# Issuing the later modulation loads of a decoder layer from GpSimd's queue instead of SyncE's

## The chip, the cores and the metric

The kernel runs on one core of one Trainium2 chip. The metric is the device time of one execution in microseconds (us). The engines are TensorE (PE), VectorE (DVE), ScalarE (ACT), GpSimd (POOL) and SyncE (SP). Loads from memory are issued by an instruction on an engine's queue and carried by the core's 16 DMA engines.

## The reference

One decoder layer (DEPTH = 1) on x of 256 tokens by D_MODEL = 2048, in fp32: a modulation from the conditioning vector c, a gated DeltaNet mixer with 16 key heads and 32 value heads of 128, a layer norm, a SwiGLU of width 5632 and a second layer norm. What matters here:

```
cond = silu(c)
mod = cond @ mod_w + mod_b                 # 2048 -> 6 * 2048
sh1, sc1, ga1, sh2, sc2, ga2 = split(mod, 6)
h = x * (1 + sc1) + sh1
y = gated_deltanet(h, w_in, ...)           # starts with h @ w_in, 2048 -> 12352
x = layer_norm(ALPHA_DN * x + (1 + ga1) * y, ...)
h = x * (1 + sc2) + sh2
y = (silu(h @ w_gate) * (h @ w_up)) @ w_down
x = layer_norm(ALPHA_DN * x + (1 + ga2) * y, ...)
```

sc1 and sh1 are needed before anything can be multiplied with w_in. Each is a product of a vector with a 2048 x 2048 matrix.

## The kernel before, in words

Every large product is made of three fp32r passes. A weight tile of 128 x 1024 (two rows of 128 inputs by 512 outputs, 512 KB) is loaded into `raw` by SP (line 187), ACT copies it to the hi half `wh` (line 190), DVE subtracts to get the lo half `wl` (line 191), and PE multiplies (lines 223 to 225). There are four buffers each of raw, wh and wl. The activations h are split in the same way into `hT` (`affine_split`, lines 375 to 391): PE transposes x (line 380), ACT makes hi (387), DVE makes the value and the lo half (390, 391).

The first part of the kernel goes in four quarters over the 2048 inputs, 512 inputs in each, so that w_in can be started before the whole of sc1 and sh1 is known. For each quarter the loop at line 884 does this, in program order:

- `mods_first(k0, ...)` computes sc1 and sh1 for the quarter's 512 columns. It has eight units u of two loads each (line 297), a load being 128 inputs by 2 x 512 columns of mod_w (128 partitions with two rows of 2 KB, 512 KB). Its products are eight small matmuls for each load (line 311); in the quarters behind the first, units 1, 3 and 5 are accumulated by DVE instead (lines 305, 307) and folded in at line 315. `to_columns` (lines 277, 280) and lines 323 and 324 then write sc1 and sh1.
- two loads of x for the quarter, 256 KB each, on SP (line 888), and `affine_split` for its four tiles of inputs;
- six chunks of w_in, one of each group in `first`: two weight loads and 24 products of 512 columns each.

The buffers of the modulation loads are borrowed from tiles that are used later: unit u takes entry u mod 5 of `early` (o2, o3, kq, kq, LA; 1 MB each, two buffers in kq). So unit 5 reuses the buffer of unit 0, and unit 0 of the next quarter that of unit 5; a load waits until PE or DVE has consumed what was in its buffer.

What is issued in which order on each queue is fixed when the program is built. A planner takes the instructions that are ready by its own estimate of durations, the one with the lowest due time first. Due times are set by hand with `at(...)`: unit u of a quarter at t0 + 1.5 u, its products at t0 + 1.5 (u + 0.5), chunk i of the same quarter's loads at t0 + 12.75 + 1 + 2 i, products of the weights from 0 on, t0 beginning at -100 and growing by 12.75 for each quarter. Due times of a quarter's chunks and of the next quarter's modulation units so overlap, and SP's queue carries them interleaved. A queue is served in order: an instruction that waits holds up all behind it.

POOL issues the loads of the small parameters (`columns`, line 143, and lines 166 and 167), and later a few loads and stores and small arithmetic. After the quarters, `mods_late` loads the other modulation weights on SP (line 332).

Of the kernel before, what the change touches and what calls it, by code (L numbers as in the profile page):

```python
# [29 lines left out]
def gdn_layer_kernel(ctx: ExitStack, tc: tile.TileContext, x, c, mod_w, mod_b, ln_g, ln_b,  # L30
                     w_gu, w_down, w_in, conv_w, a_log, dt_bias, norm_w, w_out, out):
    nc = tc.nc
# [23 lines left out]
    @contextmanager  # L56
    def at(p):

        old = tc.cur_priority
        tc.cur_priority = int((p + 200) * 1000)  # L60
        yield
        tc.cur_priority = old
# [27 lines left out]
    def tp():  # L90
        return psum.tile([128, 512], F32, name="tp", tag="tp", bufs=2)
# [41 lines left out]
    p = tp()  # L133
# [16 lines left out]
    p = tp()  # L150
# [123 lines left out]
    def to_columns(p, hw, nb):  # L274

        acc = work.tile([128, 256], F32, name="sums", tag="hf", bufs=2)
        act(acc[:, 0:hw], p[:, 0:hw], AF.Copy)
        q = tp()
        for i in range(nb):
            mm(q[:, 4 * i:4 * i + 4], acc[:, i * 128:(i + 1) * 128], ident[:, 0:128:32], start=True, stop=True)  # L280
        return q[:, 0:4 * nb].rearrange("p (i j) -> p j i", j=4)

    mod_pairs = mod_w2.rearrange("(k p) (s c) -> p k s c", p=128, c=D)

    def mods_first(k0, nk, tags, t0, gap, by_dve):


        cols, hw = nk * 128, nk * 64
        per = 1024 // cols
        p = tp()  # L290
        rest = None
        for u in range(KT // per):
            pool, tag, n = tags[u % len(tags)]
            raw = pool.tile([128, per, 2 * cols], F32, name="mraw0", tag=tag, bufs=n)
            with at(t0 + gap * u):
                for kl in range(per):
                    nc.sync.dma_start(raw[:, kl].rearrange("p (s c) -> p s c", s=2),
                                      mod_pairs[:, per * u + kl, 0:2, k0 * 128:(k0 + nk) * 128])
            with at(t0 + gap * (u + 0.5)):
                for kl in range(per):  # L300
                    k = per * u + kl
                    if u in by_dve:
                        if rest is None:
                            rest = work.tile([128, 1024], F32, name="macc", tag="macc", bufs=1)
                            ts(rest[:, 0:2 * cols], raw[:, kl], cond[:, k:k + 1], None, op0=OP.mult)
                        else:
                            stt(rest[:, 0:2 * cols], raw[:, kl], cond[:, k:k + 1], rest[:, 0:2 * cols],
                                op0=OP.mult, op1=OP.add)
                        continue
                    for j in range(4):  # L310
                        mm(p[32 * j:32 * j + 32, 0:hw], cond[:, k:k + 1].to_broadcast([128, 32]),  # L311
                           raw[:, kl, j * hw:(j + 1) * hw], start=(k == 0), stop=(k == KT - 1))
                if rest is not None and u == max(by_dve) + 1:
                    for j in range(4):
                        mm(p[32 * j:32 * j + 32, 0:hw], ones.to_broadcast([128, 32]),
                           rest[:, j * hw:(j + 1) * hw], start=False, stop=False)
        with at(t0 + gap * (KT // per)):
            qv = to_columns(p, hw, nk // 2)

            def halves(a):  # L320
                return a[:, k0:k0 + nk].rearrange("p (h i) -> p h i", h=2)

            stt(halves(sc1), qv[:, 2:4], 1.0, halves(modb[:, 16:32]), op0=OP.add, op1=OP.add)
            tt(halves(sh1), qv[:, 0:2], halves(modb[:, 0:16]), op=OP.add)
# [559 lines left out]
    for k0 in range(0, KT, 4):  # L884
        mods_first(k0, 4, early, t0, MGAP, (1, 3, 5) if k0 else ())
        with at(t0 + 8.2 * MGAP):
            for t in range(2):
                nc.sync.dma_start(xt[t][:, k0 * 128:(k0 + 4) * 128],
                                  x2[t * 128:(t + 1) * 128, k0 * 128:(k0 + 4) * 128])
        with at(t0 + 8.2 * MGAP + 0.5):  # L890
            for k in range(k0, k0 + 4, 2):
                affine_split(xt, hT, k, sc1, sh1)
        t0 += 8.5 * MGAP
        for i, group in enumerate(first):
            group.chunk(k0, t0 + CGAP0 + CGAP * i)
# [228 lines left out]
```

## Time and profile before

| | |
|---|---|
| median of 3 runs | 1728.11 us (1725.67 to 1729.37) |
| the profiled execution | 1724.8 us, span 1723.0 us |
| PE busy in the span | 1668.4 us (97%) |
| DVE, ACT, POOL busy | 1140.0, 879.3, 49.0 us |
| DMA | 390.82 MB, 227 GB/s over the span |

A view by windows gives, for each stretch, the time for which each engine was busy, the granted TensorE clock as a share of full speed, the share of time for which the DMA engines were busy (it can pass 1), and what they moved. The timeline lists instructions in order of start, with equal neighbours merged. An entry in square brackets tells how long the engine was idle before and what ended that. PEld is PE's loading of weights.

### The profile page before, as it was taken

Reading aid. Unit: us, or ns where it says so; the run is one execution under the profiler, and the core shown is the slowest. Engines: PE = TensorE matmul, PEld = TensorE weight load, DVE = VectorE, ACT = ScalarE, POOL = GpSimd, SP = SyncE. Lnnn points to the kernel's source line nnn. Section 1 sums busy time; section 2 is a strip of 40 time slices with the busy share of each in tenths; the row PEclk is TensorE's granted clock in tenths of the full one; section 3 lists DMA queues with packets and bytes.
Section 4 is the critical chain, followed back from the end, with each engine's and each line's share of the span. In section 5 each row is a group of like instructions: output and inputs, shape, how many; then the busy total and the mean of one; then the engine's idle time right before and its main releaser. Section 6 shows DMA issues by size and latency. Waiting matters only on the chain.

```text
span 1723.0 us, 23257 instructions
## 1 busy us (share of the span) xinstructions
PE 1668.4 (97%) x8685; PEld 1325.3 (77%) x8685; DVE 1140.0 (66%) x1641; ACT 879.3 (51%) x1426; POOL 49.0 (3%) x58
## 2 busy tenths in 40 slices
PE   5999999999999999999999999999999999999996
PEld 2666777787887878787788778888878887888885
DVE  2466988958966988847776865764567444455455
ACT  2433669769568667564333734444444443433331
POOL 0000000001001000000000000000000000000000
PEclk8999999999999999999999999999999999999998
DMA  9998785535863777747888576886678666765653
GB/s 351 364 337 282 225 290 186 171 111 160 257 205 112 245 247 240 247 147 237 300 285 278 159 259 193 298 271 188 187 243 290 186 190 204 249 195 190 196 193 107
DMA packets 183938, 390.82 MB, mean 227 GB/s; under 512 B 12096, under 2 KB 14320, under 8 KB 182800
## 3 DMA queue, kind: packets, MB, share of 16 engines
q1 hardware_dynamic: 181808, 378.64, 67.5%
q0 software_dynamic: 2016, 10.68, 1.8%
q8 instruction: 68, 1.11, 0.3%
q14 instruction: 46, 0.38, 0.1%
HBM read 385.08 MB, written 4.19 MB: 226 GB/s over the span
## 4 chain that ended last, share of the span: by engine, by line
PE 71%; DVE 11%; DMA 8%; issue 5%; ACT 3%; POOL 1%; SPq 1%; DVEq 0%; POOLq 0%; ACTq 0%
PE pj L224 19%; PE pj L223 19%; PE pj L225 19%; DMA mraw<-in_mod_w_dram 6%; DVE wl L191 5%; DVE macc L272 1%; PE gd L225 1%; PE gd L224 1%; ACT wh L190 1%; PE gd L223 1%; PE tp L311 1%; DVE X L586 1%; DVE cy L470 1%; DVE tmp L584 1%; PE tp L1039 1%
## 5 line engine op out<-in xcount | busy, mean ns | idle before, releaser
L191 DVE TENSOR_TENSOR wl<-raw,wh 128x1024 fp32r<-128x1024 f32 x522 | 634.9, 1222 | 375.5 <-ACT wh L190 372.4
L190 ACT ACTIVATE wh<-raw 128x1024 fp32r<-128x1024 f32 x522 | 552.3, 1061 | 603.2 <-PE pj L225 480.9
L223 PE MATMUL pj<-wh,h2T 128*128 128x512 f32 x704 | 278.2, 395 | 0.0
L225 PE MATMUL pj<-wh,h2T 128*128 128x512 f32 x704 | 276.7, 393 | 0.0
L224 PE MATMUL pj<-wl,h2T 128*128 128x512 f32 x704 | 276.6, 393 | 0.0
L223 PE MATMUL pj<-wh,hT 128*128 128x512 f32 x640 | 256.9, 403 | 0.0
L224 PE MATMUL pj<-wl,hT 128*128 128x512 f32 x640 | 256.4, 401 | 0.1
L225 PE MATMUL pj<-wh,hT 128*128 128x512 f32 x640 | 256.2, 401 | 0.0
L272 DVE SCALAR_TENSOR_TENSOR macc<-mraw,cond,macc 128x1024 f32<-128x1024 f32 x120 | 153.4, 1278 | 55.8 <-DMA mraw<-in_mod_w_dram 55.4
L223 PEld LDWEIGHTS pj<-wh,h2T 128*128 128x128 f32 x704 | 132.8, 189 | 30.7 <-issue 1.6
L225 PEld LDWEIGHTS pj<-wh,h2T 128*128 128x128 f32 x704 | 132.7, 189 | 28.6 <-issue 0.8
L224 PEld LDWEIGHTS pj<-wl,h2T 128*128 128x128 f32 x704 | 132.7, 188 | 27.5 <-issue 0.8
L223 PEld LDWEIGHTS pj<-wh,hT 128*128 128x128 f32 x640 | 120.8, 189 | 26.6 <-issue 3.3
L225 PEld LDWEIGHTS pj<-wh,hT 128*128 128x128 f32 x640 | 120.9, 189 | 24.6 <-issue 1.2
L224 PEld LDWEIGHTS pj<-wl,hT 128*128 128x128 f32 x640 | 120.8, 189 | 24.4 <-DVE wl L191 0.9
L470 DVE SCALAR_TENSOR_TENSOR cy<-tp,cw,cy 128x255 f32<-128x255 f32 (+2 forms) x192 | 86.2, 476 | 1.3 <-ACT cy L466 1.2
L224 PE MATMUL gd<-wl,hT 128*128 128x512 f32 x128 | 51.5, 404 | 1.4 <-DVE wl L191 1.4
L223 PE MATMUL gd<-wh,hT 128*128 128x512 f32 x128 | 49.9, 398 | 2.0 <-DVE part L256 1.1
L225 PE MATMUL gd<-wh,hT 128*128 128x512 f32 x128 | 51.8, 408 | 0.0
L311 PE MATMUL tp<-mraw,cond 128*32 128x256 f32 x368 | 34.9, 464 | 11.1 <-DMA mraw<-in_mod_w_dram 11.1
L223 PE MATMUL pj<-wh,oTc 128*128 128x512 f32 x112 | 43.9, 392 | 0.0
L225 PE MATMUL pj<-wh,oTc 128*128 128x512 f32 x112 | 43.8, 391 | 0.0
(385 smaller groups left out, 2252.0 us busy)
## 6 DMA issues: line engine op xcount, KB each, us to landing
raw<-in_gdn_w_in_dram SPq DMA_DIRECT2D x194, 512.0 KB, 4.7
mraw<-in_mod_w_dram SPq DMA_DIRECT2D x192, 512.0 KB, 5.4
raw<-in_ffn_w_gu_dram SPq DMA_DIRECT2D x176, 512.0 KB, 4.4
raw<-in_ffn_w_down_dram SPq DMA_DIRECT2D x88, 512.0 KB, 4.7
raw<-in_gdn_w_out_dram SPq DMA_DIRECT2D x64, 512.0 KB, 5.0
x<-in_x_dram SPq DMA_DIRECT2D x8, 256.0 KB, 6.0
r<-in_x_dram POOLq DMA_DIRECT2D x2, 1024.0 KB, 5.1
x1s<-r POOLq DMA_DIRECT2D x2, 1024.0 KB, 6.7
```

The costliest lines, as they stand in the source:

```text
L190: act(hi, raw, AF.Copy)
L191: tt(lo, raw, f32(hi), op=OP.subtract)
L223: mm(ps, sh, wh, start=start, stop=False)
L224: mm(ps, sh, wl, start=False, stop=False)
L225: mm(ps, sl, wh, start=False, stop=stop)
L272: return stt(acc, w, cond[:, k:k + 1], acc, op0=OP.mult, op1=OP.add)
L311: mm(p[32 * j:32 * j + 32, 0:hw], cond[:, k:k + 1].to_broadcast([128, 32]), raw[:, kl, j * hw:(j + 1) * hw], start=(k == 0), stop=(k == KT ...
L470: stt(y[:, o + s:o + 256], p[:, o:o + 256 - s], tap(3 - s, ct + i), y[:, o + s:o + 256], op0=OP.mult, op1=OP.add)
L584: tt(tv, LD[:, j + 1:32, j:j + 1].to_broadcast([128, n, m]), X[:, j, None, 0:m].to_broadcast([128, n, m]), op=OP.mult)
L586: tt(X[:, j + 1:32, 0:m], X[:, j + 1:32, 0:m], tv, op=OP.subtract)
L1039: tr(p[:, i * 256 + t * 128:i * 256 + (t + 1) * 128], nats[j, t][:, (2 * i2 + i) * 128:(2 * i2 + i + 1) * 128], ident)
```

## The change

The queue of the modulation loads in `mods_first` is chosen by quarter: SP for the first (k0 = 0), POOL for the three others. Sizes, buffers and due times stay, and so do all other loads.

```
+        queue = nc.gpsimd if k0 else nc.sync
         for u in range(KT // per):
             pool, tag, n = tags[u % len(tags)]
             raw = pool.tile([128, per, 2 * cols], F32, name="mraw0", tag=tag, bufs=n)
             with at(t0 + gap * u):
                 for kl in range(per):
-                    nc.sync.dma_start(raw[:, kl].rearrange("p (s c) -> p s c", s=2),
-                                      mod_pairs[:, per * u + kl, 0:2, k0 * 128:(k0 + nk) * 128])
+                    queue.dma_start(raw[:, kl].rearrange("p (s c) -> p s c", s=2),
+                                    mod_pairs[:, per * u + kl, 0:2, k0 * 128:(k0 + nk) * 128])
```

## Rows read from the trace of the kernel before

**Rows 1.** Busy time by windows: head, quarters, the rest, the span.

```profile
0.00:40.00 40.00, 22.65 (x164) 7.32 (x165) 8.15 (x22) 7.53 (x11) 4.25 (x13) 0.90 0.96 346
40.00:170.00 130.00, 126.49 (x707) 86.15 (x706) 77.86 (x88) 46.74 (x59) 0.49 (x1) 0.99 0.93 330
170.00:1723.00 1553.00, 1519.26 (x7818) 1231.78 (x7816) 1053.97 (x1532) 825.01 (x1358) 44.26 (x44) 0.99 0.67 215
sum 1723.00, PE 1668.40 PEld 1325.25 DVE 1139.98 ACT 879.29 POOL 49.01; mean PE 556.13 PEld 441.75 DVE 379.99 ACT 293.10 POOL 16.34
```

**Rows 2.** The page's chain that ended last, by engine.

```profile
PE 71%; DVE 11%; DMA 8%; issue 5%; ACT 3%; POOL 1%; SPq 1%; DVEq 0%; POOLq 0%; ACTq 0%
```

**Rows 3.** Timeline of SP's queue, head: start us, us, line, what is issued.

```profile
1.65 17.95 SPq L297 DMA_DIRECT2D mraw<-in_mod_w_dram  x16
20.50 1.62 SPq L888 DMA_DIRECT2D x<-in_x_dram  x2
25.50 0.89 SPq L297 DMA_DIRECT2D mraw<-in_mod_w_dram  x2
26.43 1.40 SPq L187 DMA_DIRECT2D raw<-in_gdn_w_in_dram  x2
```

**Rows 4.** Timeline of PE, head.

```profile
24.39 1.04 PE L311 MATMUL tp<-mraw,cond 128*32 128x256 f32 x8 [0.21 <-DMA mraw<-in_mod_w_dram]
25.67 0.64 PE L311 MATMUL tp<-mraw,cond 128*32 128x256 f32 x8 [0.25 <-DMA mraw<-in_mod_w_dram]
...
29.54 0.64 PE L311 MATMUL tp<-mraw,cond 128*32 128x256 f32 x8 [0.65 <-DMA mraw<-in_mod_w_dram]
...
31.70 1.39 PE L380 MATMUL tp<-ident,x 128*128 128x128 f32 x7 [0.25 <-DVE sh L324]
...
36.53 1.94 PE L311 MATMUL tp<-mraw,cond 128*32 128x256 f32 x16
...
38.39 1.22 PE L223 MATMUL pj<-wh,hT 128*128 128x512 f32 x2
```

**Rows 5.** Timeline of ACT and DVE, head.

```profile
34.66 1.06 ACT L190 ACTIVATE wh<-raw 128x1024 fp32r<-128x1024 f32 x1 [0.24 <-DMA raw<-in_gdn_w_in_dram]
...
35.93 1.06 ACT L190 ACTIVATE wh<-raw 128x1024 fp32r<-128x1024 f32 x1 [0.21 <-DMA raw<-in_gdn_w_in_dram]
...
36.16 0.68 DVE L391 TENSOR_TENSOR hT<-hf,hT 128x512 fp32r<-128x512 f32 x1
...
36.96 2.35 DVE L191 TENSOR_TENSOR wl<-raw,wh 128x1024 fp32r<-128x1024 f32 x2
```

**Rows 6.** DMA issues from 31 to 40 us: KB each, median us to landing.

```profile
raw<-in_gdn_w_in_dram SPq DMA_DIRECT2D x4, 512.0 KB, 10.0
mraw<-in_mod_w_dram SPq DMA_DIRECT2D x4, 512.0 KB, 10.3
prow<-in_ln_g_dram POOLq DMA_DIRECT2D x1, 16.0 KB, 4.5
prow<-in_ln_b_dram POOLq DMA_DIRECT2D x1, 16.0 KB, 4.6
```

**Rows 7.** Timeline of POOL: two places where it issues loads.

```profile
36.89 0.50 POOL L143 DMA_DIRECT2D prow<-in_ln_b_dram  x1 [0.99 <-PE tp L146]
...
1466.26 2.13 POOL L1093 DMA_DIRECT2D l<-in_ln_g_dram  x4
```

**Rows 8.** What PE waited for, 36 to 170 us: total, times, longest.

```profile
PE gd L224 <- DVE wl L191: 1.4, 3, 0.6
PE gd L223 <- DVE part L256: 1.1, 2, 0.5
...
PE gd L223 <- DMA mraw<-in_mod_w_dram: 0.5, 1, 0.5
```

**Rows 9.** Two windows of 2 us, read for granted clock and DMA share.

```profile
38.00:40.00 2.00, 2.00 (x12) 1.32 (x5) 1.98 (x3) 0.00 (x0) 0.00 (x0) 0.50 1.05 404
...
42.00:44.00 2.00, 2.00 (x10) 1.64 (x9) 1.62 (x2) 1.41 (x2) 0.00 (x0) 0.92 1.05 407
```

**Rows 10.** The chain, 60 to 170 us: first product of the second quarter.

```profile
84.46 0.45 PE pj L223 x2
```

## The prediction

> **What bounds the kernel now.** I read the busy time by stage first [rows 1]. PE is busy 1668.4 of 1723.0 us. Before 40 us it is busy 22.65 of 40, so 17.4 us are idle there; from 40 to 170 us, where all four quarters of the first projections run, 126.49 of 130, so 3.5 us are idle; and 33.7 us are idle in the 1553 us behind that, which the change does not touch. The chain that ended last is PE for 71% of the span and DMA for 8% [rows 2]. So the change can win at most the 3.5 us of the quarters and what it moves in the head, and it can lose whatever it holds PE up for.
>
> The head is bound by transfers. SP issues the 16 loads of the first quarter by 19.6 us [rows 3]; PE's products with them follow one another at the pace of landing: load 11 (counted from 0) starts at 24.39, load 12 at 25.67, load 15 at 29.54 us [rows 4]. So one load of 512 KB takes (29.54 - 24.39) / 4 = 1.29 us when all DMA engines are busy (share 1.05 at 38 to 40 us [rows 9]). Behind load 15 come the sums, the transposes of x (31.70) and, on DVE, the split of h, which ends at 36.84 [rows 4, 5]. The first weights land at 34.66 and 35.93 (ACT starts on each then), DVE has the first lo half at about 38.13, and the first product starts at 38.39 [rows 4, 5]. From there PE hardly stops: its named waits from 36 to 170 us are 1.4 us for lo halves, 1.1 us for partial sums, 0.5 us for a modulation load [rows 8], and small ones.
>
> A quarter of transfers is 16 modulation loads, 12 weight loads and 1 load's worth of x: 29 x 1.29 = 37.4 us. A quarter of PE's work runs from 38.39 [rows 4] to 84.46 us [rows 10], 46 us. Once the quarters run, PE is the slower one, and transfers have 8 us to spare in each.
>
> **The change part by part.** Nothing is added or left out: 48 of the 64 loads go to POOL's queue, their sizes and buffers stay. POOL spends 0.50 us on an issue (2.13 us for four) [rows 7]; a load here has 256 rows of 2 KB where those have 128 rows, so 0.5 to 1.1 us each, at most 53 us in the 130 us in which POOL is busy 0.49 us [rows 1]: hidden. If that cover were gone, a load would come late by 1.1 us, once. One POOL issue (36.89 us) lies beside the DVE subtraction that starts at 36.96 and takes no longer than others [rows 5, 7]. The Trainium skill warns here ("SBUF — State Buffer", Summary: rules for kernel authors): descriptors that GpSimd writes can starve while DVE runs in a two-port mode. That row does not show it; if each of 48 issues waited for one DVE instruction, it would still be hidden by POOL's idle time.
>
> SP loses 48 issues and their waits. That alone frees no time on PE where PE is not waiting; what it can give back is the part of the 3.5 us that comes from late loads: 1.4 + 0.5 = 1.9 us [rows 8]. The 1.1 us for partial sums, and the rest, hang on DVE and ACT and stay. Bounds: 0 and 3.5; I take 1.9. Of POOL's own instructions behind the moved loads, three small parameter rows come later; what is made of them is not read in the quarters.
>
> The price lies in the head. Loads of quarter two need the buffers of quarter one. In the kernel before, SP's next load waits until PE has consumed loads 10 and 11 (24.39 + 1.04 = 25.43) and is issued at 25.50, behind loads 13 to 15 and x in the same queue [rows 3, 4]. On POOL it is issued at the same moment, but it does not queue behind them. The rows show that: at 31 to 40 us, with all DMA engines busy, SP's loads took 10.0 and 10.3 us to land, POOL's two 16 KB loads 4.5 and 4.6 [rows 6]. So POOL's loads pass SP's backlog. With some 2 us of start (4.5 us to land even a small one), their bytes flow from about 27.5 us.
>
> At 27.5 us SP's queue still holds until load 15 (29.54 - 27.5 = 2.0 us alone), x (1.3 us) and two weight loads (2.6 us). Bounds of what POOL takes from it: nothing, and load 15 and x land as now (29.5, 30.8); everything it has, six loads (units 0 and 1, whose buffers are released by then, and unit 2, which waits for no later one), 6 x 1.29 = 7.7 us. Packets on both are 2 KB rows, so I take half of the pace for each: load 15 lands at 27.5 + 4.1 = 31.6 (2.1 late), x at 27.5 + 6.6 = 34.1 (3.3 late), the two weight loads at 36.7 and 39.3. The transposes need x and then go 3.3 us later, DVE's split of h ends at 40.1, and the first product starts at 38.39 + 3.3 = 41.7. PE's 1.86 us with unit 0 just ahead of it fill the wait as now. No row of before has two large queues side by side, so the half is an estimate between those bounds.
>
> The Trainium skill has a rule for just this ("DMA: Bandwidth & Descriptors", Queues, rings and completion order): each DMA engine serves the queues it has work for in turn, packet by packet. The 4.5 us agree with it as far as they go; by it the sum would be the one made here, with the bounds of nothing and of 7.7 us it would be -1.9 and +5.8 us.
>
> At 38 to 40 us the granted clock is 0.50 (1.2 GHz), at 42 to 44 us 0.92 [rows 9]; PE was half idle before. The later start moves this low stretch as a whole, which costs nothing more; if it ends no later than now, 3 us at half clock become 3 us at full clock, a gain under 1.5 us that I leave to the range.
>
> Sum: +3.3 - 1.9 = +1.4 us on the profiled execution, 1724.8 + 1.4 = 1726.2. The median shown, 1728.11, stands 3.3 us above that execution, so the forecast is 1728.11 + 1.4 = 1729.5 us. A measurement of this kernel tells about 0.2% (3.5 us) from no change, so this is "same".
>
> **The rivals.** (a) Forecast: the head pays 3.3, the quarters give 1.9 back. Chance 0.36.
>
> (b) No effect: bytes land in the order in which they were issued, or POOL's start is so late that load 15 and x are through; and the small waits stay, being DVE's. 0 to +1 us, 1728.6. For it: PE, not SP, bounds the quarters. Against it: 4.5 against 10 us [rows 6]. The Trainium skill ("DMA: Bandwidth & Descriptors", Issuing engines are not separate DMA queues) speaks for it: all queues run on the same engines, and a second one only saves issue time. Issue time is on nobody's path here. Chance 0.14.
>
> (c) Faster: POOL takes little at first. Then SP's first weight loads, which now stand behind two loads of quarter two and were held until 25.43, go out right behind x at 22 us and land 2 x 1.29 = 2.6 us sooner; DVE fits the first lo half around the split of h, and products start at 37.1 rather than 38.39, 1.3 us won. With 1.9 to 3.5 us of waits gone the gain is 3.2 to 4.8, say 4.0: 1724.1. It decides when POOL's first bytes come after load 15, at 29.5 us. Chance 0.17.
>
> (d) Slower: PE waits for loads in the wrong order. PE's program is one fixed order, made when the program is built, in which products with modulation loads outrank those of the weights (the 16 of unit 0 stand ahead of the first product [rows 4]). If five buffers, 10 loads, are put ahead of the second chunk because the planner lets them land early, they land at 27.5 + 10 x 2.58 = 53.3 us; PE, starting at 41.7 and needing some 7 us for the first chunk (part of it at low clock), would be there at 49 and wait 4.3 us. With the head's 3.3 it is +7.6, less 0 to 1.9 given back: 1735 us. Later quarters would not repeat it, as transfers have 8 us to spare in each. It decides when PE's second chunk has more than four units ahead of it. A POOL that takes all it can in the head (+5.8) ends nearly there. Chance 0.33.
>
> **How the numbers follow.** Likeliest is (a), 1729.5. Its own range, with POOL's share between a third and two thirds, is 1727 to 1732. (a) and (b) are within 0.2% (1724.7 to 1731.6) but for a small part that the runs' own scatter moves out on either side. Faster 0.18, same 0.48, slower 0.34. From 1723 (all of (c)) to 1737 (all of (d), with a little more) about 2 in 10 is left out, most of it above: a longer wait in (d), or a planned order that differs later in the kernel too.
>
> **What would show it.** SP's queue: the two x loads are followed at once by four weight loads, near 22 us. POOL's queue: the first moved load near 25.5 us. Load 15's products start near 31.6 (now 29.54), the first transposes of x near 34.5, the first weight product near 41.7. If these are at 29.5 and 37, (c) is right. PE idle from its first weight product to 170 us falls to about 1.6 us; a wait there of PE for a modulation load, of several us before 60, is (d). Landing of moved loads at about 10 us or more and of weight loads at 5 to 10. The stage behind 170 us should keep its 1553 us. The prediction is wrong if POOL's issues take over 2.8 us each, if its loads land one after the other, or if the order of PE's work changes behind the quarters.

## The result and the profile after

The changed kernel takes 1752.95 us (median of 4 runs, 1749.45 to 1756.03) against 1728.44 us for the kernel before (four runs of it; the 1728.11 us ahead of the prediction are the median of three): ratio 1.0154, 95% interval 1.0126 to 1.0181. It is slower by about 24 us; the forecast was +1.4 us and its range ended at 1737.

The profiled execution takes 1752.09 us. Lines from 291 on have moved down by two (L311 is now L313, L380 is L382, L888 is L890). First the windows, as in [rows 1]:

```profile
0.00:40.00 40.00, 20.44 (x142) 5.88 (x142) 2.04 (x12) 5.42 (x9) 10.32 (x21) 0.87 0.96 346
40.00:170.00 130.00, 122.03 (x671) 91.97 (x675) 83.44 (x94) 49.26 (x56) 28.13 (x41) 0.92 0.93 337
170.00:1750.30 1580.30, 1532.92 (x7880) 1239.93 (x7872) 1056.62 (x1536) 828.53 (x1363) 49.00 (x45) 0.99 0.66 211
sum 1750.30, PE 1675.39 PEld 1337.78 DVE 1142.10 ACT 883.21 POOL 87.45; mean PE 558.47 PEld 445.93 DVE 380.70 ACT 294.40 POOL 29.15
```

The span of the profiled execution grew by 1750.3 - 1723.0 = 27.3 us, 3 us more than the medians. PE's idle time against [rows 1] grew by 19.56 - 17.35 = 2.2 us before 40 us, by 7.97 - 3.51 = 4.5 us in the quarters and by 47.4 - 33.7 = 13.6 us behind them; the other 7.0 us are busy time (1675.4 against 1668.4) for the same products, which I put down to the clock: from 40 to 170 us the granted clock is 0.92, not 0.99. Half of the loss lies behind 170 us, in a stage that the diff does not touch; 3.6 us of it come before 200 us, where quarter four's modulation now ends.

The chain that ended last by engine [rows 2], DMA at 11% where it had 8%:

```profile
PE 65%; DMA 11%; DVE 10%; issue 8%; ACT 4%; POOL 1%; SPq 0%; DVEq 0%; POOLq 0%; ACTq 0%
```

SP's queue in the head, against [rows 3]:

```profile
20.20 1.62 SPq L890 DMA_DIRECT2D x<-in_x_dram  x2
22.75 6.76 SPq L187 DMA_DIRECT2D raw<-in_gdn_w_in_dram  x4
```

POOL's timeline, the first moved loads and the last:

```profile
22.91 1.44 POOL L299 DMA_DIRECT2D mraw<-in_mod_w_dram  x2 [18.04 <-PE tp L313]
25.51 4.24 POOL L299 DMA_DIRECT2D mraw<-in_mod_w_dram  x6 [1.16 <-PE tp L313]
...
118.31 1.42 POOL L299 DMA_DIRECT2D mraw<-in_mod_w_dram  x2 [2.23 <-DVE macc L309]
167.90 0.52 POOL L143 DMA_DIRECT2D prow<-in_gdn_norm_w_dram  x1 [48.17 <-PE tp L146]
168.93 1.44 POOL L299 DMA_DIRECT2D mraw<-in_mod_w_dram  x2 [0.51 <-PE tp L313]
```

SP does issue four weight loads from 22.75 us, as foretold. POOL starts at 22.91, 2.6 us sooner than the 25.5 that was forecast, and has issued eight loads by 29.75. What to see further down: a parameter row (L143) stood in POOL's queue for 48 us until PE transposed an earlier row out of its buffer, and the last unit's loads stood behind it.

PE's head, against [rows 4]:

```profile
26.66 0.64 PE L313 MATMUL tp<-mraw,cond 128*32 128x256 f32 x8 [0.21 <-DMA mraw<-in_mod_w_dram]
29.23 0.64 PE L313 MATMUL tp<-mraw,cond 128*32 128x256 f32 x8 [1.94 <-DMA mraw<-in_mod_w_dram]
32.81 1.08 PE L313 MATMUL tp<-mraw,cond 128*32 128x256 f32 x8 [2.94 <-DMA mraw<-in_mod_w_dram]
...
36.60 1.54 PE L382 MATMUL tp<-ident,x 128*128 128x128 f32 x6 [0.34 <-DMA x<-in_x_dram]
...
41.52 1.20 PE L223 MATMUL pj<-wh,hT 128*128 128x512 f32 x2
...
44.02 0.80 PE L224 MATMUL pj<-wl,hT 128*128 128x512 f32 x1 [0.64 <-DVE wl L191]
```

The last three loads of quarter one come 2.57 and 3.58 us apart instead of 1.29. The transfers from 31 to 40 us, against [rows 6], with the two queues' packets, MB and share:

```profile
q0 software_dynamic: 669, 2.47, 67.1%
q1 hardware_dynamic: 666, 1.28, 36.6%
...
mraw<-in_mod_w_dram POOLq DMA_DIRECT2D x2, 512.0 KB, 11.8
x<-in_x_dram SPq DMA_DIRECT2D x2, 256.0 KB, 17.9
```

POOL's queue (q0) and SP's (q1) got the same number of packets, 669 and 666, but POOL's carry 3.7 KB and SP's 1.9 KB on average: POOL takes two thirds. That agrees with the rule of the Trainium skill ("DMA: Bandwidth & Descriptors", Queues, rings and completion order) that a DMA engine takes the queues it has work for in turn, a packet at a time, if the packets that the profile counts are those of the rule, which no run here shows. Equal turns were not equal bytes.

ACT's start on each of the first two weight loads [rows 5], 5.5 and 7.9 us later than before:

```profile
40.20 1.06 ACT L190 ACTIVATE wh<-raw 128x1024 fp32r<-128x1024 f32 x1 [0.72 <-DMA raw<-in_gdn_w_in_dram]
43.84 1.06 ACT L190 ACTIVATE wh<-raw 128x1024 fp32r<-128x1024 f32 x1 [2.58 <-DMA raw<-in_gdn_w_in_dram]
```

DVE's order changed too. Quarter two's first accumulation (L307) now stands ahead of quarter one's split of h (L392, L393), and DVE waited 4 us in it for a moved load:

```profile
39.66 0.75 DVE L307 TENSOR_SCALAR macc<-mraw,cond 128x1024 f32<-128x1024 f32 x1 [3.99 <-DMA mraw<-in_mod_w_dram]
...
42.75 1.22 DVE L191 TENSOR_TENSOR wl<-raw,wh 128x1024 fp32r<-128x1024 f32 x1
43.88 0.68 DVE L393 TENSOR_TENSOR hT<-hf,hT 128x512 fp32r<-128x512 f32 x1
```

In the kernel before, that accumulation stood behind the first two lo halves and started at 39.23 us. Here the first lo half starts at 42.75, 1.5 us after ACT had its hi half (40.20 + 1.06), so this order can have cost some 1.5 us (an estimate from these rows).

The granted clock by windows; in [rows 9] it is 0.92 from 42 us:

```profile
44.00:50.00 6.00, 5.98 (x14) 4.74 (x15) 4.89 (x5) 3.00 (x3) 1.63 (x3) 0.50 1.04 404
50.00:60.00 10.00, 8.95 (x45) 6.96 (x48) 7.24 (x9) 4.25 (x4) 1.42 (x2) 0.99 1.04 386
```

PE is busy all through 44 to 50 us, at 1.2 GHz. PE's waits from 36 to 170 us, against [rows 8]: the old ones are nearly gone, and new ones are longer.

```profile
PE tp L317 <- DVE macc L309: 4.6, 1, 4.6
PE tp L146 <- issue: 3.3, 1, 3.3
PE tp L313 <- DVE cw L147: 1.1, 1, 1.1
PE pj L224 <- DVE wl L191: 0.6, 1, 0.6
```

On PE's and then DVE's timeline, the places of quarters two and four:

```profile
59.62 3.66 PE L313 MATMUL tp<-mraw,cond 128*32 128x256 f32 x64 [1.05 <-DVE cw L147]
...
72.23 1.08 PE L317 MATMUL tp<-macc,upper 128*32 128x256 f32 x8 [4.64 <-DVE macc L309]
...
177.07 1.08 PE L317 MATMUL tp<-macc,upper 128*32 128x256 f32 x8 [2.94 <-DVE macc L309]
```

```profile
59.28 0.48 DVE L147 COPY cw<-tp 128x128 f32<-128x128 f32 x2
...
174.03 1.28 DVE L309 SCALAR_TENSOR_TENSOR macc<-mraw,cond,macc 128x1024 f32<-128x1024 f32 x1 [5.77 <-DMA mraw<-in_mod_w_dram]
```

Before, the products with modulation loads came in many small lots; now 64 of the 80 in quarter two and again in quarter four stand in one lot, in quarter two behind the copies of a parameter column (`cw`). In quarter four the fold (L317) waits for an accumulation whose load was issued at 168.93, behind the parameter row. The order of the built program says the same; it counts the products of w_in that PE does ahead of each lot of modulation products:

```
            quarter two                quarter four
before      0,20,30,54,59,91,...105,110  288 to 398 in lots
after       52 (four of five PE units)   420 (four of five PE units)
```

### The profile page after: what moved, and what is told of

It is laid out like the page before. It is cut to its first block, busy times and chain, and to the rows that moved or that the text cites. A ratio compares the mean times of both kernels' runs of the same rounds, so it can differ in the third digit from the quotient of the medians.

```text
span 1750.3 us, 23260 instructions
## 1 busy us (share of the span) xinstructions
PE 1675.4 (96%) x8685; PEld 1337.8 (76%) x8685; DVE 1142.1 (65%) x1641; ACT 883.2 (50%) x1428; POOL 87.4 (5%) x106
## 4 chain that ended last, share of the span: by engine, by line
PE 65%; DMA 11%; DVE 10%; issue 8%; ACT 4%; POOL 1%; SPq 0%; DVEq 0%; POOLq 0%; ACTq 0%
PE pj L223 18%; PE pj L225 18%; PE pj L224 18%; DMA mraw<-in_mod_w_dram 8%; DVE wl L191 4%; DMA raw<-in_gdn_w_in_dram 2%; DVE cy L472 1%; PE gd L224 1%; PE gd L223 1%; PE gd L225 1%; ACT wh L190 1%; DVE macc L272 1%; PE tp L1041 1%; ACT tp L503 1%; PE tp L313 1%
## 5 line engine op out<-in xcount | busy, mean ns | idle before, releaser
L225 PE MATMUL pj<-wh,hT 128*128 128x512 f32 x640 | 260.3, 407 | 0.4 <-DVE hT L393 0.4
L223 PE MATMUL pj<-wh,hT 128*128 128x512 f32 x640 | 260.1, 407 | 0.1
L223 PEld LDWEIGHTS pj<-wh,hT 128*128 128x128 f32 x640 | 122.8, 192 | 25.1 <-issue 1.2
L225 PEld LDWEIGHTS pj<-wh,hT 128*128 128x128 f32 x640 | 122.7, 192 | 24.7 <-DVE hT L393 0.8
L313 PE MATMUL tp<-mraw,cond 128*32 128x256 f32 x368 | 33.4, 482 | 15.0 <-DMA mraw<-in_mod_w_dram 14.0
L223 PE MATMUL pj<-wh,oTc 128*128 128x512 f32 x112 | 43.9, 392 | 0.0
L224 PE MATMUL pj<-wl,oTc 128*128 128x512 f32 x112 | 43.8, 391 | 0.1
```

Source lines behind the costliest of these rows:

```text
L223: mm(ps, sh, wh, start=start, stop=False)
L224: mm(ps, sh, wl, start=False, stop=False)
L225: mm(ps, sl, wh, start=False, stop=stop)
```

## The experiments

Three theories stood at first. *Head*: POOL's loads pass SP's and everything up to the first weights comes late. *Order*: the planner, with loads no longer in SP's single line, builds a worse order, for which two places offered themselves, the parameter columns and the due times of the modulation products. *Transfers*: the moved loads take the DMA engines from weights that are needed sooner, in every quarter. The expectations call *order* P where it means the columns and Q where it means the due times, and *transfers* C.

**One part of the change alone (e3, e4), the columns (e1, e2).** e3 moves quarter two alone, e4 quarters three and four; e1 is the changed kernel with the columns' transposes and copies due at once, e2 the kernel before with the same edit.

```
-        queue = nc.gpsimd if k0 else nc.sync
+        queue = nc.gpsimd if k0 == 4 else nc.sync     # e3
+        queue = nc.gpsimd if k0 > 4 else nc.sync      # e4
```

```
+            with at(-99.0):                           # e1, e2
                 p = tp()
                 tr(p[:, :n], r[:n], ident[:n, :n])
                 nc.vector.tensor_copy(o, p[:, :n])
```

> The changed kernel, with the transposes and copies of the small parameter columns given the lowest due time (-99), so that they never hold one of the two tp banks while weight products or weight splits go ahead of them. Theory P (priority inversion in the planned order: a column transpose or its copy holds a tp bank, the quarter's modulation products can't start, buffers of the modulation loads stay full, and its last loads come late): the waits of PE for the folding of macc (7.6 us) go, the total falls by more than half of the 24.5 us lost, to 1728 to 1738, what remains being the head. Theory C (POOL's loads take DMA time from the weights and x): the loads still run ahead, so the total stays at 1745 or more.

> The kernel before with the same due time for the columns: a control. Both theories: no change, 1725 to 1732. If it is slower by over 5 us, the columns' due time itself costs and e1 is to be read against this.

> Only the second quarter's modulation loads on POOL. The built order still puts all of the second quarter's products with modulation weights behind 52 weight products, as in the changed kernel, but those of the fourth quarter no longer in a heap. Theory P: about half of the loss stays, 1737 to 1745 (the head's 3 us, the wait near 70 us and the low clock around it). Theory C: a third of the loads, a third of the loss plus the head, 1736 to 1740. So it tells little between them by its total; the wait of PE for macc near 70 us, 4 to 5 us, is what P asks for and C does not.

> Only the third and fourth quarters' loads on POOL, so that nothing passes the first quarter in the head. If the head is what costs (first weight product at 41.5 instead of 38.4 us), the first product is back at 38.4 and 3 to 5 us of the loss go from it. Theory P: the built order heaps the products of both quarters (4 x 8 at a time) but the fourth no longer stands behind 420 weight products: 1732 to 1742. Theory C: two thirds of the loads, 1740 to 1745.

Measured against before: e1 1.0118 [1.0096, 1.0140], e2 1.0002 [0.9987, 1.0017], e3 1.0102 [1.0073, 1.0131], e4 1.0127 [1.0102, 1.0151]. Neither half of the change is harmless and the halves do not add up to the whole. The columns cost nothing in the kernel before and some 6 us after the change (the intervals of e1 and of the changed kernel overlap a little). None of this fits P alone: e1 stands where C put it, e3 within P's range and e4 above both. e1 also let the next flaw through: all quarters' modulation products now run far ahead, and PE waits for their loads, as one of several such rows of PE's timeline shows:

```profile
56.30 0.64 PE L314 MATMUL tp<-mraw,cond 128*32 128x256 f32 x8 [2.78 <-DMA mraw<-in_mod_w_dram]
```

**Due times of the products (r1 to r4).** The products of the moved units are given due times that follow the weights' products.

```
-            with at(t0 + gap * (u + 0.5)):
+            with at(pos[0] - 6 + 0.65 * u if k0 else t0 + gap * (u + 0.5)):
```

r1 is the changed kernel with this, r2 has the columns' edit too, r3 is r2 with quarter two back on SP, r4 has both edits and all loads on SP.

> The changed kernel with the products of the modulation units of quarters two to four given due times among the weight products of the quarter before (0.65 of a chunk apart), so that they use up their buffers, and thereby release the next loads, at a steady pace. Columns as in the changed kernel. Theory Q (the shared queue of SP had paced the loads; on POOL only the buffers do, and the planner puts all products with them far ahead, where PE waits for them): part of the loss goes, but the built order still has all of the fourth quarter's products behind 420 weight products because a column holds a tp bank, so +8 to +18 us over before. Theory C (POOL's loads take DMA time whatever the order): no change against the changed kernel, +22 to +27.

> Pacing of the products and the low due time of the columns together, all 48 loads on POOL. The built order then has the modulation products at nearly the same places among the weight products as the kernel before. Theory Q: PE's waits for them between 50 and 170 us go, what is left is the head, where POOL's loads pass the last ones of the first quarter and x: +3 to +8 us. Theory C: as the loads are the same, +15 or more.

> As the last, but the second quarter's loads stay on SP, so that nothing passes the first quarter either. Theory Q: level with before, -3 to +3 us. Theory C: two thirds of the loads still on POOL, +10 or more.

> Control: the kernel before, all loads on SP, with both due-time edits. The built order is nearly that of before. Both theories: -3 to +3 us.

Measured: r1 1.0184 [1.0169, 1.0200], r2 1.0105 [1.0079, 1.0132], r3 1.0058 [1.0042, 1.0074], r4 1.0014 [1.0001, 1.0027]. Pacing by itself did not help (r1 against 1.0154, r2 against e1's 1.0118): the due times were not the cause, and r1, r2 and r3 are all slower than Q allowed. The columns were part of it: r1 to r2 is 12 us. PE's idle time from 170 to 960 us tells where, by windows of r1 and of r2, in this order:

```profile
170.00:960.00 790.00, 761.28 (x4479) 610.77 (x4478) 607.93 (x1076) 497.82 (x1003) 38.40 (x29) 0.99 0.66 210
```

```profile
170.00:960.00 790.00, 773.57 (x4493) 622.20 (x4483) 612.95 (x1081) 502.81 (x1007) 33.01 (x26) 0.99 0.67 213
```

28.7 us idle without the columns' edit and 16.4 with it, as many as in r4 (15.8). Some 3 of these 12 us lie before 200 us, where the late loads are waited for; the other 9 lie behind, and no run ties them to one wait. POOL's timeline of r1 and of r2 shows the hold:

```profile
173.01 0.52 POOL L143 DMA_DIRECT2D prow<-in_gdn_norm_w_dram  x1 [26.47 <-PE tp L146]
174.05 1.44 POOL L299 DMA_DIRECT2D mraw<-in_mod_w_dram  x2 [0.51 <-PE tp L313]
```

```profile
137.99 0.53 POOL L143 DMA_DIRECT2D prow<-in_gdn_norm_w_dram  x1 [1.49 <-PE tp L147]
...
144.72 1.42 POOL L300 DMA_DIRECT2D mraw<-in_mod_w_dram  x2 [0.28 <-DVE macc L310]
```

What is left is 0.9% between r2 and r4. PE is idle there for 31.6 us up to 170 us in r2 and 18.8 in r4, and behind 170 us about as long in one as in the other (36.3 and 37.0).

**The head back on SP, fewer buffers (s1 to s3).** s1 is r2 with units 0 to 4 of quarter two on SP; s2 is r3 with three borrowed buffers in quarters three and four; s3 is both.

```
+            queue = nc.gpsimd if k0 > 4 or k0 and u >= 5 else nc.sync          # s1, s3
...
+        mods_first(k0, 4, early if k0 <= 4 else early[:3], t0, ...)            # s2, s3
```

> Kernel r2 (both edits, all 48 loads on POOL, 1.0105) with one thing undone: units 0 to 4 of quarter two, the 10 loads that can start while the first quarter is still landing, go back to SP; units 5 to 7 and quarters three and four stay on POOL. Theory 'passing in the head': those 10 loads are what makes the first weights and x late, and they alone are the difference of 10 us between r2 and r3. Then x is transposed near 32 us and the first weight product is near 38.5 us as before, the half clock ends near 42 us, PE is idle some 15 us before 40 and 60 us (r2: 20.5 and 24.5), and the time is that of r3: 1.004 to 1.007 of before. Rival 'share': each load on POOL costs about the same wherever it stands; then 38 of 48 loads leave about four fifths of r2's loss, 1.008 to 1.009.

> Kernel r3 (both edits, only quarters three and four on POOL, 1.0058) with three borrowed buffers instead of five in quarters three and four, so that POOL can be at most six loads ahead of PE and not ten. PE's built order hardly differs. Theory 'running ahead': POOL has nothing in its queue that holds it back but buffers, takes half of the DMA engines as soon as five are free, and SP's weight loads land late; with three buffers the waits of PE for lo halves fall (r3: 5.4 us in three rows) and the time is 1.002 to 1.004. Rival 'just in time': fewer buffers make the modulation loads late; PE waits for them for over 5 us and the time is 1.006 or more. If neither waits move and the time stays at 1.005 to 1.006, the loss is not in the transfers of the quarters but in the order behind them.

> Kernel s1 with three borrowed buffers in quarters three and four: the repair of the head and that of running ahead together, 38 of the 48 loads on POOL. If both theories hold, the losses add up and their repairs too: 1.002 to 1.004, within 3 us of s2 and within 4 us of the control r4 (1.0014). If the head theory falls, it is at 1.007 or more whatever s2 does; if only running ahead falls, it stands where s1 stands.

Measured: s1 1.0093 [1.0071, 1.0115], s2 1.0054 [1.0036, 1.0071], s3 1.0081 [1.0064, 1.0098]. The head theory was expected to explain the whole step from r3 to r2 and did not. The head itself came back, with the first weight product at 39.48 us (r2 41.97, r4 39.78). PE's idle time up to 170 us fell by 7 us (31.6 to 24.6 by the windows), the profiled spans differ by 4.6 us (1743.4 and 1738.8), and the ratios by 2 us, with intervals of 4 us on either side. How much of the head's loss comes back later is thus only known to within a few us. Running ten loads ahead or six made no difference either (s2 against r3). DVE's timeline of s1, then PE's, shows a new place:

```profile
81.99 0.75 DVE L308 TENSOR_SCALAR macc<-mraw,cond 128x1024 f32<-128x1024 f32 x1 [4.82 <-DMA mraw<-in_mod_w_dram]
85.22 1.28 DVE L310 SCALAR_TENSOR_TENSOR macc<-mraw,cond,macc 128x1024 f32<-128x1024 f32 x1 [2.48 <-DMA mraw<-in_mod_w_dram]
86.43 0.15 DVE L326 SCALAR_TENSOR_TENSOR sc<-tp,modb 128x4 f32<-128x4 f32 x1
```

```profile
86.80 0.63 PE L383 MATMUL tp<-ident,x 128*128 128x128 f32 x4 [3.46 <-DVE sh L327]
```

The next quarter's accumulation stands on DVE ahead of this quarter's scale and shift, and waits for loads; PE waits for the shift.

**That order on DVE undone (v1 to v3).** One DVE instruction of 4 columns, which reads the shift and the accumulator, keeps the next accumulation behind the shift in quarters two to four; the first quarter has no accumulator, so its head is left as it was. It is added to s1, r2 and s2.

```
             tt(halves(sh1), qv[:, 0:2], halves(modb[:, 0:16]), op=OP.add)
+            if rest is not None:
+                tie = work.tile([128, 4], F32, name="tie", tag="tie", bufs=1)
+                tt(tie, rest[:, 0:4], sh1[:, k0:k0 + 4], op=OP.add)
```

> Kernel s1 (38 of 48 loads on POOL, 1.0093) with one DVE instruction of 4 columns added behind each quarter's shift, which reads the shift and the accumulator, so that the next quarter's accumulation can only be built behind them. No load moves to another queue. Theory 'order on DVE': scale and shift no longer stand behind loads that land late; PE's waits for the shift (5.3 us in two rows in s1) fall below 1 us, with them the half clock around 80 to 90 us, and the time falls by 4 to 8 us, to 1.005 to 1.007. Rival 'transfers': the waits only change their name (to lo halves or to modulation loads) and the time stays at 1.008 to 1.010.

> Kernel r2 (all 48 loads on POOL, both edits, 1.0105) with the same DVE instruction. Theory 'order on DVE': r2 has 5.4 us of waits for the shift, which go; with the half clock behind them 5 to 8 us: 1.006 to 1.008, and the difference to v1 is then what the passing in the head costs by itself (idle of PE up to 60 us: r2 24.5, s1 16.8). Rival 'transfers': 1.009 to 1.011.

> Kernel s2 (only quarters three and four on POOL, three buffers there, 1.0054) with the same DVE instruction. PE waits in s2 for a lo half (2.9 us in one row near 80 us) because DVE stands at an accumulation whose load is late; the tie holds that accumulation back only until the shift, so theory 'order on DVE' expects part of it: 1.002 to 1.005. Rival 'transfers': no change, 1.005 to 1.006.

Measured: v1 1.0093 [1.0073, 1.0113], v2 1.0113 [1.0089, 1.0136], v3 1.0090 [1.0069, 1.0110]. The waits for the shift are gone in v1 and v2, and the time is not: they took other names. So accumulations ahead of the later shifts are not the cause of what is left. In v2's head DVE still waits in quarter two's first accumulation, ahead of the split of h, until 41.76 us; in v1 it does not, and v1 is still 0.8% above r4. v3 is even slower than s2, which neither theory expected and I have not explained. ACT's timeline of v2 shows what the engines come to stand at:

```profile
92.38 1.06 ACT L191 ACTIVATE wh<-raw 128x1024 fp32r<-128x1024 f32 x1 [8.01 <-DMA raw<-in_gdn_w_in_dram]
```

The DMA issues from 60 to 100 us, of r4 (all on SP) and then of r2 (all on POOL), say why; the last column is the median time to landing.

```profile
mraw<-in_mod_w_dram SPq DMA_DIRECT2D x16, 512.0 KB, 7.6
raw<-in_gdn_w_in_dram SPq DMA_DIRECT2D x12, 512.0 KB, 5.6
```

```profile
mraw<-in_mod_w_dram POOLq DMA_DIRECT2D x12, 512.0 KB, 9.2
raw<-in_gdn_w_in_dram SPq DMA_DIRECT2D x10, 512.0 KB, 12.4
```

The weights are not just issued sooner: the 13th of them is issued at 69.65 us in r4 and at 69.07 in r2, and lands at 74.28 and 85.99.

**Half the bytes (h1 to h3).** h1, h2 and h3 are r2, r4 and r3 with half the bytes in each load behind the first quarter; they leave out the scale there. PE's built order is then almost one and the same in all three (4 of some 7,000 lines differ between h3 and h2, 19 between h1 and h2).

```
+                    if k0:
+                        queue.dma_start(raw[:, kl, 0:cols],
+                                        mod_pairs[:, per * u + kl, 0, k0 * 128:(k0 + nk) * 128])
+                        continue
...
-                           raw[:, kl, j * hw:(j + 1) * hw], ...
+                           raw[:, kl, (j % 2 if k0 else j) * hw:((j % 2 if k0 else j) + 1) * hw], ...
```

> Kernel r2 (both edits, all 48 loads on POOL) with half the bytes: each load behind the first quarter brings only the shift's 512 columns (256 KB), and the products and sums for the scale are made from the same half, so the scale is left out and the work on PE and DVE keeps its count. Its control is h2, the same on SP. With whole loads the two stand 0.9% apart (r2 1.0105, r4 1.0014). Theory 'transfers': the loss goes with the bytes that pass the weights, so h1 is 0.2 to 0.5% over h2, the first weight product some 1.5 us later than in h2 and not 3, and the half clock shorter. Rival 'built order': PE's order is the same in h1 and h2, so they agree within 0.15%. Rival 'queue': 48 issues on POOL cost the same whatever they bring, 0.8 to 1.0%.

> Control of h1 and h3: kernel r4 (both edits, all loads on SP) with half the bytes behind the first quarter; the scale is left out there. 48 loads of 256 KB less, 12 MB or 48 x 0.65 = 31 us of full transfer, which PE hardly waits for: 0.999 to 1.002 of before.

> Kernel r3 (both edits, quarters three and four on POOL) with half the bytes; the scale is left out behind the first quarter. With whole loads r3 stands 0.44% over r4. Theory 'transfers': at half the bytes SP's weights have room, 0 to 0.2% over h2. Rival 'queue': 0.4%. Rival 'built order' (PE's is the same as in h2 but for four lines): within 0.1%; this run alone does not tell that from 'transfers', h1 does.

Measured: h1 1.0044 [1.0029, 1.0058], h2 0.9990 [0.9978, 1.0003], h3 1.0009 [0.9995, 1.0022]. With whole loads POOL cost 0.91% (r2 over r4) and 0.44% (r3 over r4); with half the bytes it costs 0.54% (h1 over h2), just above what 'transfers' expected, and 0.19% (h3 over h2). By the intervals the 0.91% is known to some 0.3% and the 0.54% to some 0.2%, so that the one is smaller than the other is barely clear of the scatter. Windows of h2 and of h1, quarters:

```profile
40.00:170.00 130.00, 128.84 (x744) 93.46 (x737) 91.11 (x119) 47.99 (x59) 0.49 (x1) 1.00 0.82 268
```

```profile
40.00:170.00 130.00, 126.39 (x719) 90.90 (x720) 85.16 (x113) 50.65 (x61) 20.71 (x39) 0.97 0.74 252
```

The built order of PE being the same, it can't make the difference between h1 and h2. A fixed price of an issue on POOL would not have shrunk; that the loss goes with the bytes that pass the weights is the reading that fits best. It is not the only one, as DVE's order differs between h1 and h2. PE's and DVE's timelines of h1:

```profile
34.42 1.02 PE L281 MATMUL tp<-ident,sums 128*128 128x4 f32 x4 [0.50 <-ACT sums L278]
```

```profile
35.27 0.88 DVE L313 TENSOR_SCALAR macc<-mraw,cond 128x512 f32<-128x512 f32 x2 [31.40 <-DMA mraw<-in_mod_w_dram]
...
37.04 0.16 DVE L333 SCALAR_TENSOR_TENSOR sc<-tp,modb 128x4 f32<-128x4 f32 x1
```

The sums come 3.1 us later than in h2 (31.29), behind a wait of 2.58 us for load 15, which is the transfers; the scale then comes 1.6 us after them, behind accumulations of quarter two, which in h2 start at 40.87 us, behind the scale and the first lo halves. How much of the 0.54% is that order's is open. h2 tells one more thing: 12 MB less on SP's queue gave 0.1% against the kernel before and 0.24% against r4, its like with whole loads. In due order the kernel hardly waits for these transfers, so there was little for any queue to win, and no kernel here that does the whole work beats the one before.

## Why the prediction was wrong

- **What PE's limit is, and that at most 3.5 us could be won**: right as far as h2 can tell, where 12 MB less gave 4 us against r4. Of the 1.9 us to be given back, the named waits did shrink (lo halves from 1.4 to 0.6 us, the partial sums' and the load's rows are gone). It was paid for with others.
- **The price of an issue on POOL, hidden**: right; 0.71 us each (4.24 us for six), and POOL is busy 28.1 of 130 us.
- **The head**: the mechanism was right and the sum came out by luck. The first weight product is at 41.52 us, forecast 41.7. But load 15 came at 32.81 (31.6), x at about 36.6 (34.1) and the first two weight loads at 40.2 and 43.8 (36.7 and 39.3): the mis-sized term is "Packets on both are 2 KB rows, so I take half of the pace for each". POOL's packets were 3.7 KB on average and it took two thirds; it also started 2.6 us sooner, with eight loads before load 15 landed where the sum had six. The split of h ended at 44.6 (40.1), as it stood behind quarter two's accumulation on DVE. What hid it: the 16 products of unit 0 that stood ahead of the first weight product (36.53 to 38.39 us in [rows 4]) had been built elsewhere, so "PE's 1.86 us with unit 0 just ahead of it" fell away. The first product reads only hi halves, and it came behind the weights' first one (41.26) and a column's transpose (41.42), not behind x and the whole split.
- **"The later start moves this low stretch as a whole, which costs nothing more"**: failed. The half clock lasted to about 50 us, 8 us longer than before, while the first product came 3.1 us later. The weights behind the first one were late too, so PE stopped again (first product with a lo half at 44.02, before at 39.41). PE is busy 7.0 us longer in all for the same products, which I put down to the clock here and after later pauses (0.54 from 70 to 80 us); no run isolates it. I had given no price to a wait beyond its own length.
- **"Once the quarters run, PE is the slower one, and transfers have 8 us to spare in each"**: this is the step that failed most. It is true as a sum of bytes and says nothing on their order. The DMA engines were busy 0.93 of 40 to 170 us before as well [rows 1], because loads run ahead as far as buffers allow. On one queue those loads stand behind the weights of an earlier due time. On a second queue they pass them: from 60 to 100 us weights take 12.4 us to land in r2 where they take 5.6 in r4. By PE's idle time up to 170 us (31.6 against 18.8) this and the head are most of the 0.9%, some 15 us, between those two.
- **What POOL's queue was holding, and "the 1553 us behind that, which the change does not touch"**: failed. That stretch took 1580.3 us, in part because work of the quarters had moved into it, and PE was idle there for 13.6 us more. The sentence "three small parameter rows come later; what is made of them is not read in the quarters" looked at the rows behind the loads and missed the loads behind the rows. A row's load waits until PE has transposed an earlier row out of the buffer, which PE did at 167.4 us. That was harmless as long as nothing stood behind it. Together with PE's modulation products standing behind those columns it cost 12 us (r1 to r2), nearly all of it behind 170 us. Which of the waits there hangs on which stays open. That the stage "should keep its 1553 us" was the prediction's own sign, and it did not.
- **Rival (d)** named the right kind, an order built on loads that are thought to land early, and placed it too narrowly: "Later quarters would not repeat it" was wrong: PE waited 4.6 us for an accumulation in quarter two and 2.9 in quarter four. Rivals (b) and (c) fell with the first rows of the head. The Trainium skill's sentence for (b) ("DMA: Bandwidth & Descriptors", Issuing engines are not separate DMA queues), that a second queue saves issue time only, holds for the rate, which stayed (417 against 407 GB/s at 31 to 40 us); the time shows that it also changes who is served first.

Shown by experiments: the columns' share, that POOL's queue costs 0.54% where PE's built order is the same, and that accumulations ahead of a shift or of the split of h are not needed for the loss (v1). Argued, from the landing times and from h1 over h2: that this cost goes with the bytes. Not settled: what DVE's order adds where it does change, how the rest divides between the head and the later quarters (2 to 5 us for the head's ten loads, by s1), and why v3 is slower than s2.

## What to carry to other kernels

A queue that several streams share is also the order among them: loads that have time should stay behind those that are due, and moving them to a second queue lets them take bandwidth from the first (here two thirds of it, with packets of twice the size), whatever the total leaves to spare. Before moving loads onto a queue, read what already waits in it and on whom, for every load behind that inherits the wait. Price a wait on TensorE with the stretch at half clock behind it, and expect a planner to rebuild the order of every engine when a load changes its queue.

## What the runs showed of the hardware

- Two queues with work on the same DMA engines got equal numbers of packets (669 and 666 in 9 us; 676 and 675 in e1), at 3.7 and 1.9 KB, hence bytes of two to one.
- POOL took 0.71 us to issue a load of 512 KB in 256 rows, against 0.50 us for the small rows of [rows 7], and such loads landed in 7.7 to 11.8 us (medians of several stretches).
- After a head with PE half idle, PE ran at 1.2 GHz through 44 to 50 us although it was busy 5.98 of those 6 us.
